# A hybrid encoder block: branch B's tiles at fixed places in the stream of projections, and four heads' meta keys as one block

## The chip, the cores and the metric

The kernel runs on one core of one Trainium2 chip. The metric is device time in microseconds (us), from the start of the program to its end. TensorE multiplies matrices, VectorE and ScalarE work on tiles in SBUF and PSUM, GpSimd on tiles in SBUF, and SyncE's queue (SP) issues all the DMAs. In the profile PE is TensorE's matmuls, PEld its weight loads, DVE VectorE, ACT ScalarE and POOL GpSimd.

## The reference

`x` has 1024 tokens of width 1024 in float32; 16 learned meta tokens are put in front, so the sequence has 1040. One layer:

```
hn     = rms_norm(h)                                   # h = [meta, x]
proj   = hn @ w_in                                     # qa ka va (512 each) qb (512) kb vb (128 each) ga gb (1024 each)
y_a    = differential attention, 4 heads, over all 1040 keys, ALiBi bias
y_b    = windowed attention, 8 query heads on 2 key/value heads of width 64 (4 heads share one):
         each query sees the 16 meta keys and the real keys within 128 positions;
         softmax with a learned sink in the denominator
merged = sigmoid(ga) * (y_a @ w_ba) + sigmoid(gb) * (y_b @ w_bb)
h      = h + merged @ w_o
h      = h + (silu(hn2 @ w_gate) * (hn2 @ w_up)) @ w_down      # hn2 = rms_norm(h), d_ff 2816
out    = rms_norm(h)[16:]
```

The change concerns `y_b` and the projections around it.

## The kernel before, in words

Float32 values are split into a high and a low part (`split`: ScalarE copies the high part, VectorE or GpSimd subtracts), and a product is three matmuls: high by high, high by low, low by high.

**The stream of projections.** `project_steps` makes 128 columns of `proj` from transposed, normed tokens (`hT_hi`, `hT_lo`), in chunks of tokens. One step is three matmuls for one of eight blocks of the contraction; after the eighth, the chunk leaves PSUM (three banks, tag `pp`). A chunk of qa has 512 tokens (16 steps for 1024). The chunks of va and ka have 384, 384 and 272 (24 steps), in ka of the last head 272 first. `prep` loads and splits a weight block; `ensure(n)` sees that n blocks are prepared ahead. The V projections pass through `vt` and are transposed later, four blocks of 128 tokens at a time (`turning_v`, one call every eight steps of the next projection). The order is kb, the first half of qb, vb; then qa, va, ka of heads 0 and 1; the second half of qb; qa, va, ka of heads 2 and 3.

**Branch B.** Group g (0 and 1) has four heads and eight tiles of 128 queries. `attend_b(g, t, qb)` does one tile:
- Scores: for each of its four heads two matmuls into PSUM (`bps`, two banks). The keys are up to three blocks of 128, each with the 16 meta keys behind it: 432 columns, at the edge tiles (0 and 7) 288. VectorE adds the bias and takes the minimum (`bmn`), ScalarE takes Exp and sums (`bdn`), VectorE adds the sink and takes the reciprocal, and GpSimd scales the four heads by it (L343).
- GpSimd copies the meta columns, twice side by side, into `md`, a zeroed tile with 128 columns for each head (`bmd`, L347).
- `finish`: for each key block four transposes, one for each head, into PSUM (`bpt`), ScalarE's high copy and VectorE's low one (`btr`), and two value matmuls of 512 columns (four heads by 128 queries) into `bpy`. Then the meta block in the same way: four transposes of `md`, a high and a low copy side by side in rows 0 to 31, and one value matmul with block 8 of `vb`, which holds V of the meta keys twice. The result is added up and stored to `yb_d`.

`units_b` writes tile t + 1's scores ahead of tile t's `finish`.

**Order.** Most of the program is ordered by a planner, which lays the instructions of each engine on a simulated timeline and takes those written first first. In `manual_schedule(engines=...)` an engine keeps the order in which the program is written. Before, GpSimd is in hand order from the second half of qb to the first gate weights, and TensorE from branch A on. Ahead of that the planner chose: it put pieces of branch B between matmuls of the projections by itself.

**Beside it on GpSimd.** `token_sums(c)` forms, for c from 0 to 3, ten sums of 128 by 512 of the tokens for the gate products (a Strassen scheme), and `keep` splits and stores four of them (`ts_d`). `weight_sums(n)` forms four sums of gate weights of 128 by 256 and stores them (`ws_d`), two calls for each tile of group 1 (`sums_of`).

After the last projection come the first gate products (L717, 72 matmuls of 512 columns), and then branch A's attention with the other gate products between its tiles (L737, L796).

Of the kernel before, what the change touches and what calls it, by code (L numbers as in the profile page):

```python
# [9 lines left out]
F32 = mybir.dt.float32  # L10
# [9 lines left out]
P = 128  # L20
# [53 lines left out]
def encoder_block(ctx: ExitStack, tc: tile.TileContext, x, meta, norm_mix, w_in, lq1, lk1, lq2, lk2,  # L74
# [7 lines left out]
    def f32(ap):  # L82
        return ap.bitcast(F32)
# [13 lines left out]
    def bank(p, tag, name, bufs):  # L97
        return p.tile([P, 512], F32, tag=tag, name=name, bufs=bufs)
# [140 lines left out]

    def project_v(col, name, evac):  # L240
        vt = vtpool.tile([P, L + NM], F32, tag="vt", name=f"vt_{name}", bufs=1)
        project(col, K_CHUNKS, name, lambda ps, at, n: nc.scalar.copy(vt[:, at:at + n], ps))
        nc.vector.tensor_copy(vt[:, L:L + NM], vt[:, S:L])

        def turn():
            for b in range(3):
                nb = 4 if b < 2 else 1
                kp = P if b < 2 else 2 * NM
                pt = pp_bank(f"pv_{name}_{b}").rearrange("p (c t) -> p c t", c=4)
                for i in range(nb):  # L250
                    k = 4 * b + i
                    nc.tensor.transpose(pt[:kp, i, :], vt[:, k * P:k * P + kp], ident)
                evac(pt[:kp, :nb, :], 4 * b, nb, kp)
                yield

        turning_v[:] = [turn()]
# [13 lines left out]
    vb = [(bpool if g else vtpool).tile([P, 9, P], F32R, tag=("q1", "vb")[g], name=f"vb{g}", bufs=1) for g in range(BG)]  # L270
    mds = [bpool.tile([P, 4, P], F32, name=f"bmd{i}") for i in range(2)]
    for i in range(2):
        nc.gpsimd.memset(f32(vb[i])[:, 8, :], 0.0)
        nc.gpsimd.memset(mds[i], 0.0)

# [32 lines left out]

    def project_qb(g, qb):
        for jj in range(2):  # L310
            ensure(1)
            for _ in qb_steps(g, qb, jj):
                pass
            ensure(W_BUFS - 1)

    def attend_b(g, t, qb):
        nm = f"{g}_{t}"
        b0, b1 = max(t - 1, 0), min(t + 2, NT)
        nb = b1 - b0
        W = nb * 144  # L320
        j0 = b0 - t + 1
        tb = tbx[:, j0:j0 + nb, :].rearrange("p j k -> p (j k)")
        st = bpool.tile([P, 4, 432], F32, tag="bs", name=f"bs_{nm}", bufs=2)
        mn = small.tile([P, 4], F32, tag="bmn", name=f"bmn_{nm}")
        dn = small.tile([P, 4], F32, tag="bdn", name=f"bdn_{nm}")
        es = small.tile([P, 4], F32, tag="bes", name=f"bes_{nm}")
        hs = slice(4 * g, 4 * g + 4)
        for r in range(4):
            ps = bank(psum1, "bs", f"bps_{nm}_{r}", 2)
            for v in range(2):  # L330
                nc.tensor.matmul(ps[:, :W], qb[:, r, t * P:(t + 1) * P],
                                 kb[g][:, v, b0:b1, :].rearrange("p b k -> p (b k)"), start=(v == 0), stop=(v == 1))
            nc.vector.tensor_tensor_reduce(st[:, r, :W], ps[:, :W], tb, 2.0 ** -(4 * g + r + 1), nsink[:, 4 * g + r:4 * g + r + 1],
                                           ALU.add, ALU.min, mn[:, r:r + 1])
        nc.vector.tensor_tensor(es, mn, sinkb[:, hs], ALU.add)
        for r in range(4):
            nc.scalar.activation(st[:, r, :W], st[:, r, :W], AF.Exp, bias=mn[:, r:r + 1], scale=-1.0,
                                 accum_out=dn[:, r:r + 1])
        nc.scalar.activation(es, es, AF.Exp)
        nc.vector.tensor_tensor(dn, dn, es, ALU.add)  # L340
        nc.vector.reciprocal(dn, dn)  # L341
        for r in range(4):
            nc.gpsimd.tensor_scalar(st[:, r, :W], st[:, r, :W], dn[:, r:r + 1], 1.0, ALU.mult, ALU.mult)  # L343

        md = mds[t % 2]
        own = (t - b0) * 144 + P
        nc.gpsimd.tensor_copy(md[:, :, 0:2 * NM].rearrange("p r (a k) -> p r a k", a=2),  # L347
                              st[:, :, own:own + NM].unsqueeze(2).broadcast_to([P, 4, 2, NM]))

        def finish():  # L350
            py = bank(psum1, "by", f"bpy_{nm}", 1)
            blocks = [(k, P, (k - b0) * 144) for k in range(b0, b1)] + [(8, P, (t - b0) * 144 + P)]
            for k, kp, o in blocks:
                pt = bank(psum1, "bt", f"bpt_{nm}_{k}", 2).rearrange("p (r t) -> p r t", r=4)
                for r in range(4):
                    nc.tensor.transpose(pt[:kp, r, :], st[:, r, o:o + P] if k < 8 else md[:, r], ident)  # L356
                tr = bpool.tile([P, 2, 4, P], F32R, tag="btr", name=f"btr_{nm}_{k}", bufs=4)
                nc.scalar.activation(tr[:kp, 0], pt[:kp], AF.Copy)
                lo = tr[:, 1] if k < 8 else tr[:NM, 0]
                nc.vector.tensor_tensor(lo, pt[:lo.shape[0]], f32(tr[:lo.shape[0], 0]), ALU.subtract)  # L360
                for hl in range(2 if k < 8 else 1):
                    nc.tensor.matmul(py, vb[g][:kp, k, :], tr[:kp, hl].rearrange("p r t -> p (r t)"),  # L362
                                     start=(k == b0 and hl == 0), stop=(k == 8))
# [5 lines left out]
        return finish  # L369

# [91 lines left out]
    early += [(p_kb, DC), (p_q0, DC), (p_q1, DC)]  # L462
    advance(100)
    dist = acon.tile([P, 1920], F32, name="dist")
    tbx = acon.tile([P, 3, 144], F32, name="tbx")
# [34 lines left out]


    first_b = [attend_b(0, t, qb) for t in range(2)]
    project_v(C_VB, "vb", vb_evac)
    flush_v()
# [5 lines left out]
    def token_sums(c):  # L510
# [16 lines left out]
        tt(t1, t1, low, ALU.add)  # L527
        keep(5, t1)
        t3, t2 = new(3), new(2)
        tt(t3, part(0, 1, 1), part(0, 0, 1), ALU.subtract)  # L530
        tt(t2, part(1, 1, 1), part(1, 0, 1), ALU.subtract)
        tt(t3, t3, t2, ALU.add)
        keep(7, t3)
        tt(t2, t3, part(0, 0, 0), ALU.add)
        tt(t2, t2, part(1, 0, 0), ALU.add)
        keep(6, t2)
        t4 = new(4)
        tt(t4, part(0, 1, 0), t2, ALU.subtract)
# [3 lines left out]
    def project_a(h):  # L542
# [16 lines left out]

        project(C_QA + h * P, Q_CHUNKS, f"qa{h}", evac_split(-(2.0 ** (2 * h - 1)), q_consume))  # L560
        project_v(C_VA + h * P, f"va{h}", va_evac)
        project(C_KA + h * P, K_CHUNKS if h < AH - 1 else K_CHUNKS[::-1], f"ka{h}", evac_split(None, k_consume))

    def units_b(g, qb, pending=(), extra=lambda t: None):
        pending = list(pending)
        for t in range(len(pending), NT):
            if len(pending) > 1:
                pending.pop(0)()
            pending.append(attend_b(g, t, qb))
            extra(t)  # L570
            if len(pending) > 1:
                pending.pop(0)()
        for p in pending:
            p()


    def load_sums(p, kh, half):
# [99 lines left out]

    order_pool = tc.manual_schedule(engines={mybir.EngineType.Pool})
    order_pool.__enter__()
    qb = new_qb(1)  # L680
    project_qb(1, qb)
    for n in range(2):
# [9 lines left out]

    units_b(1, qb, extra=sums_of)
    close_bpool()
# [187 lines left out]

    order_pe = tc.manual_schedule(engines={mybir.EngineType.PE})
    order_pe.__enter__()
    tiles, turning, tail = [], iter(()), []
# [626 lines left out]
```

## Time and profile before

| | |
|---|---|
| runs | 1446.01, 1449.07, 1449.72 us (median 1449.07) |
| profiled execution | 1446.1 us, span 1444.3 us |
| granted TensorE clock | 0.997 |
| busy, share of the span | TensorE 99%, weight loads 85%, VectorE 62%, ScalarE 47%, GpSimd 44% |
| normed tokens, kb and the first half of qb | up to 56 us |
| vb, both groups of branch B, the projections of branch A | 56 to 305 us, the last value matmul of branch B at 309.9 us |
| first gate products | to 322.9 us |
| branch A's attention and all that follows | to 1444.3 us |

The rows of a timeline have start, length, engine, line, operation, output<-inputs, shape and count; in brackets stands the idle time of the engine just before, with what ended it. The rows of groups have count, then busy us and mean ns, then idle us before them and what ended most of it. A mean length of a matmul is longer than its pace, since matmuls overlap.

### The profile page before, as it was taken

Reading aid. Unit: us, or ns where it says so; the run is one execution under the profiler, and the core shown is the slowest. Engines: PE = TensorE matmul, PEld = TensorE weight load, DVE = VectorE, ACT = ScalarE, POOL = GpSimd, SP = SyncE. Lnnn points to the kernel's source line nnn. Section 1 sums busy time; section 2 is a strip of 40 time slices with the busy share of each in tenths; the row PEclk is TensorE's granted clock in tenths of the full one; section 3 lists DMA queues with packets and bytes.
Section 4 is the critical chain, followed back from the end, with each engine's and each line's share of the span. In section 5 each row is a group of like instructions: output and inputs, shape, how many; then the busy total and the mean of one; then the engine's idle time right before and its main releaser. Section 6 shows DMA issues by size and latency. Waiting matters only on the chain.

```text
span 1444.3 us, 21160 instructions
## 1 busy us (share of the span) xinstructions
PE 1422.8 (99%) x7279; PEld 1221.2 (85%) x7279; DVE 899.2 (62%) x1624; ACT 679.6 (47%) x1290; POOL 641.3 (44%) x605
## 2 busy tenths in 40 slices
PE   8999999999999999999999999999999999999997
PEld 6988989988898999888888878888888888888886
DVE  7478536637697989624614966554555553787567
ACT  6366535545665656544413643333333333444454
POOL 5599127743333333334522665544544452000444
PEclk9999999999999999999999999999999999999999
DMA  8467658986557473576612534333332332964443
GB/s 244 90 209 237 193 162 265 288 281 213 190 169 257 147 227 125 190 256 209 216 34 88 152 104 161 109 102 110 102 102 96 110 102 102 331 208 140 124 129 139
DMA packets 188891, 242.41 MB, mean 168 GB/s; under 512 B 18208, under 2 KB 115936, under 8 KB 188784
## 3 DMA queue, kind: packets, MB, share of 16 engines
q1 hardware_dynamic: 188784, 241.07, 52.6%
q8 instruction: 57, 0.93, 0.3%
q14 instruction: 50, 0.41, 0.1%
HBM read 157.45 MB, written 77.00 MB: 162 GB/s over the span
## 4 chain that ended last, share of the span: by engine, by line
PE 81%; POOL 6%; DVE 5%; issue 4%; DMA 2%; ACT 1%; POOLq 0%; SPq 0%; DVEq 0%; ACTq 0%
PE pg L1293 28%; PE pd L1387 9%; PE pg L737 7%; PE po L1070 6%; PE ppa L780 6%; PE aps L796 3%; PE pp_qb L214 3%; POOL oa L118 3%; PE apy L835 3%; PE pp_ka L214 2%; PE pp_va L214 2%; PE apt L822 2%; PE pp_qa L214 2%; PE bpt L356 1%; PE bpy L362 1%
## 5 line engine op out<-in xcount | busy, mean ns | idle before, releaser
L118 POOL TENSOR_TENSOR wop<-wf,wop 128x512 fp32r<-128x512 f32 x128 | 172.6, 1353 | 165.5 <-ACT wop L117 149.6
L1293 PE MATMUL pg<-t,wop 128*128 128x512 f32 x1056 | 242.6, 389 | 0.0
L1293 PEld LDWEIGHTS pg<-t,wop 128*128 128x128 f32 x1056 | 198.3, 188 | 41.1
L1387 PE MATMUL pd<-ob,oa 128*128 128x512 f32 x924 | 209.9, 389 | 0.4 <-POOL oa L118 0.4
L1387 PEld LDWEIGHTS pd<-ob,oa 128*128 128x128 f32 x924 | 173.4, 188 | 36.8 <-POOL oa L118 0.8
L1293 PE MATMUL pg<-b,wop 128*128 128x512 f32 x792 | 185.6, 392 | 2.3 <-DVE c L1302 2.3
L1293 PEld LDWEIGHTS pg<-b,wop 128*128 128x128 f32 x792 | 149.5, 189 | 34.1 <-issue 2.4
L737 PE MATMUL pg<-hT_hi,gop 128*128 128x512 f32 x384 | 142.7, 396 | 0.0
L118 POOL TENSOR_TENSOR oa<-ra,oa 128x512 fp32r<-128x512 f32 x33 | 44.0, 1335 | 170.1 <-ACT oa L117 168.6
L117 ACT ACTIVATE wop<-wf 128x512 fp32r<-128x512 f32 x128 | 80.2, 631 | 82.9 <-PE pg L1293 48.6
L118 POOL TENSOR_TENSOR gop<-gr,gop 128x512 fp32r<-128x512 f32 x48 | 63.3, 1319 | 116.4 <-ACT gop L117 102.6
L117 ACT ACTIVATE oa<-ra 128x512 fp32r<-128x512 f32 x77 | 48.7, 632 | 105.9 <-PE pd L1387 45.1
L804 ACT ACTIVATE as<-as,amn 128x1040 f32<-128x1040 f32 x64 | 74.5, 1164 | 46.9 <-DVE amn L799 42.8
L1128 DVE TENSOR_TENSOR s<-wf,wf 128x512 f32<-128x512 f32 x22 | 25.0, 1138 | 108.1 <-DMA wf<-in_w_ff_gate_dram 58.0
L796 PE MATMUL aps<-ak,aq 128*128 128x392 f32 (+1 forms) x384 | 90.0, 330 | 1.3 <-DVE amn L799 0.6
L1070 PE MATMUL po<-woh,mT 128*128 128x512 f32 x384 | 88.0, 390 | 0.0
L1070 PEld LDWEIGHTS po<-woh,mT 128*128 128x128 f32 x384 | 71.9, 188 | 14.8
L796 PEld LDWEIGHTS aps<-ak,aq 128*128 128x128 f32 x384 | 69.6, 189 | 15.0 <-DVE amn L799 2.2
L737 PEld LDWEIGHTS pg<-hT_hi,gop 128*128 128x128 f32 x384 | 72.7, 189 | 11.2 <-DVE gk L742 0.2
L343 POOL TENSOR_SCALAR bs<-bs,bdn 128x432 f32<-128x432 f32 (+1 forms) x64 | 41.4, 666 | 85.5 <-DVE bdn L341 73.4
L737 PE MATMUL pg<-hT_lo,gop 128*128 128x512 f32 x192 | 76.0, 396 | 0.0
L807 POOL TENSOR_SCALAR as<-as,adn,neglam 128x1040 f32<-128x1040 f32 x32 | 38.8, 1214 | 62.5 <-DVE adn L805 43.9
(287 smaller groups left out, 3099.0 us busy)
## 6 DMA issues: line engine op xcount, KB each, us to landing
ra<-aop SPq DMA_DIRECT2D x77, 256.0 KB, 2.6
wf<-in_w_ff_gate_dram SPq DMA_DIRECT2D x24, 512.0 KB, 4.0
wf<-in_w_ff_up_dram SPq DMA_DIRECT2D x24, 512.0 KB, 3.9
aop<-as SPq DMA_DIRECT2D x44, 256.0 KB, 2.1
w_c<-in_w_in_dram SPq DMA_DIRECT2D x17, 512.0 KB, 5.7
aop<-c SPq DMA_DIRECT2D x33, 256.0 KB, 2.0
ts_d<-to SPq DMA_DIRECT2D x16, 512.0 KB, 3.7
gw<-in_w_in_dram SPq DMA_DIRECT2D x32, 256.0 KB, 3.9
```

The source lines that it names most:

```text
L117: nc.scalar.activation(hi, src, AF.Copy)
L118: lo_eng.tensor_tensor(lo, src, f32(hi), ALU.subtract)
L214: nc.tensor.matmul(ps[:, :n], a[:, c, :], b[:, c, at:at + n], start=(c == 0 and i == 0), stop=(c == DC - 1 and i == 2))
L343: nc.gpsimd.tensor_scalar(st[:, r, :W], st[:, r, :W], dn[:, r:r + 1], 1.0, ALU.mult, ALU.mult)
L737: nc.tensor.matmul(ps, op[:, a, c], quad(b, *act)[:, c], start=(p in (2, 5, 1) and c == 0 and i == 0), stop=(p in (2, 3, 4) and c == 3 and ...
L780: nc.tensor.matmul(ps, w[:, a, j, :], src(j, b, tk), start=(j == 0 and n == 0), stop=(j == 3 and n == 2))
L796: nc.tensor.matmul(ps[:, :n], qs[m][:, t * P:(t + 1) * P], ks[m][:, vv, k0:k0 + n], start=(vv == 0), stop=(vv == 1))
L804: nc.scalar.activation(s[m][:, 0:L], s[m][:, 0:L], AF.Exp, bias=low, scale=-1.0, accum_out=dn[:, m:m + 1])
L835: nc.tensor.matmul(py[:, cols], v[:kp, a, k, :], at_[:kp, k, b, :], start=(k == 0 and j == 0), stop=(k == 8))
L1070: nc.tensor.matmul(ps, mT[:, c, a, t * P:(t + 1) * P], wos[q, c][:, b], start=(c == 0 and n == 0), stop=(c == DC - 1 and n == 2))
L1293: nc.tensor.matmul(ps, op[:, x, c, :], b[:, y, c, :], start=(p in (1, 2, 5) and c == 0 and n == 0), stop=(p in (4, 2, 3) and c == 3 and n ...
L1387: nc.tensor.matmul(ps[u], oa[:, a, u * P:(u + 1) * P], ob[:, b, :], start=(p in (1, 2, 5) and j == 0 and k == 0), stop=(p in (2, 3, 4) and ...
```

## The change

1. TensorE keeps the written order from the vb projection on, and so does GpSimd. The planner still orders VectorE, ScalarE and SP.
2. `project`, `project_v`, `project_qb` become `stream`, `stream_v`, `stream_qb`, which yield after each step. `ensure` for the next weights comes in the fourth step rather than at the end.
3. `attend_b` returns two generators. `scores` yields after each head (and takes Exp of a head right behind its minimum); `turns` yields after each piece: first the transpose of the meta block and of the first key block; then for each further block its four transposes and the values of the block before; last the values of the last block and of the meta block, and the store.
4. `plan(g, t, base)` lays a tile's scores at steps base - 14, -12, -10, -8 of the stream and its pieces at base, + 4, + 8 and (inner tiles) + 12. Group 0 has base 16t + 4 from the first step of qa of head 0 on, its first tile's scores lying in steps 12 to 18 of vb; group 1 has base 182 + 13t. `along` walks the streams, 288 steps in all, and calls what is due.
5. `token_sums` yields after each kept sum, and its 16 pieces lie at steps 5, 13, 21 and so on. The weight sums of tile t lie at step 182 + 13t - 7.
6. Group 1's tiles are written among the projections of heads 2 and 3, no longer ahead of them. The vb transposes are called at once behind vb, as before.
7. `md` holds, for the four heads, 32 columns each (the 16 meta columns twice), 128 in all: one transpose for the tile. The result is copied to SBUF, and for head r the rows 32r to 32r + 31 go into columns of head r of `diag`, an otherwise zeroed tile: a high copy by ScalarE, and a low one by VectorE over the first 16 of these rows. Block 8 of `vb` holds V of the meta keys eight times (`vb_meta`), and one matmul over 128 rows gives all four heads.

```diff
-    def project(col, chunks, name, evac):
+    def stream(col, chunks, name, evac):
         ensure(1)
         for i, _ in enumerate(project_steps(col, chunks, name, evac)):
             if i % DC == V_AT and turning_v:
                 next(turning_v[0], None)
-        ensure(W_BUFS - 1)
+            if i == 3:
+                ensure(W_BUFS - 1)
+            yield
...
+        if name == "vb":
+            meta = bpool.tile([P, P], F32, tag="by1", name="vb_meta", bufs=2)
+            nc.vector.tensor_copy(meta.rearrange("p (a k) -> p a k", a=8), vt[:, S:L].unsqueeze(1).broadcast_to([P, 8, NM]))
...
     def attend_b(g, t, qb):
...
+        def scores():
...
+            for r in range(4):
+                nc.gpsimd.tensor_scalar(st[:, r, :W], st[:, r, :W], dn[:, r:r + 1], 1.0, ALU.mult, ALU.mult)
+            md = held["md"] = bpool.tile([P, 4, 2, NM], F32, tag="bmd", name=f"bmd_{nm}", bufs=2)
+            nc.gpsimd.tensor_copy(md, st[:, :, own:own + NM].unsqueeze(2).broadcast_to([P, 4, 2, NM]))
+            yield
+
+        def turns():
+            st, md, dg, trs = held["st"], held["md"], diag[:, t % 2], {}
...
+            pt = bank(psum1, "bt", f"bpt_{nm}_8", 2)[:, 0:P]
+            nc.tensor.transpose(pt, md.rearrange("p r a k -> p (r a k)"), ident)
+            sc = bpool.tile([P, P], F32, tag="bsc", name=f"bsc_{nm}", bufs=2)
+            nc.scalar.copy(sc, pt)
+            turn(b0)
+            for r in range(4):
+                hi, lo = slice(32 * r, 32 * r + 32), slice(32 * r, 32 * r + NM)
+                nc.scalar.activation(dg[hi, r], sc[hi], AF.Copy)
+                nc.vector.tensor_tensor(dg[lo, r], sc[lo], f32(dg[lo, r]), ALU.subtract)
+            yield
+            for k in range(b0 + 1, b1):
+                turn(k)
+                value(k - 1)
+                yield
+            value(b1 - 1)
+            nc.tensor.matmul(py, vb[g][:, 8, :], dg.rearrange("p r t -> p (r t)"), start=False, stop=True)
...
-    first_b = [attend_b(0, t, qb) for t in range(2)]
-    project_v(C_VB, "vb", vb_evac)
+    order_pe = tc.manual_schedule(engines={mybir.EngineType.PE})
+    order_pe.__enter__()
+    order_pool = tc.manual_schedule(engines={mybir.EngineType.Pool})
+    order_pool.__enter__()
+    diag = bpool.tile([P, 2, 4, P], F32R, tag="bys", name="diag", bufs=1)
+    nc.gpsimd.memset(f32(diag), 0.0)
+    tiles_b = {(0, t): attend_b(0, t, qb) for t in range(NT)}
+    for i, _ in enumerate(stream_v(C_VB, "vb", vb_evac)):
+        if i in (12, 14, 16, 18):
+            next(tiles_b[0, 0][0])
     flush_v()
...
+    def plan(g, t, base, scores=True):
+        sc, tu = tiles_b[g, t]
+        for i in range(4 if scores else 0):
+            events.setdefault(base - 14 + 2 * i, []).append(sc)
+        for i in range(4 if 0 < t < NT - 1 else 3):
+            events.setdefault(base + 4 * i, []).append(tu)
...
-    units_b(0, qb, first_b)
-    for c in range(2):
-        token_sums(c)
-    project_a(0)
-    token_sums(2)
-    project_a(1)
-    token_sums(3)
+    for t in range(NT):
+        plan(0, t, 16 * t + 4, t > 0)
+    pieces = [token_sums(c) for c in range(4)]
+    for n in range(16):
+        extras[8 * n + 5] = lambda g=pieces[n // 4]: next(g, None)
+    along(project_a(0))
+    along(project_a(1))
...
-    units_b(1, qb, extra=sums_of)
+    for t in range(NT):
+        tiles_b[1, t] = attend_b(1, t, qb)
+        plan(1, t, 182 + 13 * t)
+        extras[182 + 13 * t - 7] = lambda t=t: sums_of(t)
+    along(project_a(2))
+    along(project_a(3))
     close_bpool()
...
-    project_a(2)
-    project_a(3)
```

More of the change, by code (lines that the diff above doesn't have):

```diff
@@ L251, in turn @@
                     k = 4 * b + i
-                    nc.tensor.transpose(pt[:kp, i, :], vt[:, k * P:k * P + kp], ident)
+                    nc.tensor.transpose(pt[:kp, i, :], vt[:, k * P:k * P + kp] if b < 2 else meta, ident)
                 evac(pt[:kp, :nb, :], 4 * b, nb, kp)
@@ L318, in attend_b @@
         b0, b1 = max(t - 1, 0), min(t + 2, NT)
-        nb = b1 - b0
-        W = nb * 144
+        W = (b1 - b0) * 144
         j0 = b0 - t + 1
[L322 to L343, printed above, removed]
@@ L345, in attend_b @@
-        md = mds[t % 2]
-        own = (t - b0) * 144 + P
-        nc.gpsimd.tensor_copy(md[:, :, 0:2 * NM].rearrange("p r (a k) -> p r a k", a=2),
-                              st[:, :, own:own + NM].unsqueeze(2).broadcast_to([P, 4, 2, NM]))
-        def finish():
+        own = (t - b0) * 144 + P
+        held = {}
+        def scores():
+            tb = tbx[:, j0:j0 + b1 - b0, :].rearrange("p j k -> p (j k)")
+            st = held["st"] = bpool.tile([P, 4, 432], F32, tag="bs", name=f"bs_{nm}", bufs=2)
+            mn = small.tile([P, 4], F32, tag="bmn", name=f"bmn_{nm}")
+            dn = small.tile([P, 4], F32, tag="bdn", name=f"bdn_{nm}")
+            es = small.tile([P, 4], F32, tag="bes", name=f"bes_{nm}")
+            for r in range(4):
+                ps = bank(psum1, "bs", f"bps_{nm}_{r}", 2)
+                for v in range(2):
+                    nc.tensor.matmul(ps[:, :W], qb[:, r, t * P:(t + 1) * P],
+                                     kb[g][:, v, b0:b1, :].rearrange("p b k -> p (b k)"), start=(v == 0), stop=(v == 1))
+                nc.vector.tensor_tensor_reduce(st[:, r, :W], ps[:, :W], tb, 2.0 ** -(4 * g + r + 1), nsink[:, 4 * g + r:4 * g + r + 1],
+                                               ALU.add, ALU.min, mn[:, r:r + 1])
+                nc.scalar.activation(st[:, r, :W], st[:, r, :W], AF.Exp, bias=mn[:, r:r + 1], scale=-1.0,
+                                     accum_out=dn[:, r:r + 1])
+                if r < 3:
+                    yield
+            nc.vector.tensor_tensor(es, mn, sinkb[:, 4 * g:4 * g + 4], ALU.add)
+            nc.scalar.activation(es, es, AF.Exp)
+            nc.vector.tensor_tensor(dn, dn, es, ALU.add)
+            nc.vector.reciprocal(dn, dn)
+            for r in range(4):
[3 more added lines that the diff above has]
+            yield
@@ L351, in finish, with turn, value @@
+        def turns():
+            st, md, dg, trs = held["st"], held["md"], diag[:, t % 2], {}
             py = bank(psum1, "by", f"bpy_{nm}", 1)
-            blocks = [(k, P, (k - b0) * 144) for k in range(b0, b1)] + [(8, P, (t - b0) * 144 + P)]
-            for k, kp, o in blocks:
+            def turn(k):
+                o = (k - b0) * 144
                 pt = bank(psum1, "bt", f"bpt_{nm}_{k}", 2).rearrange("p (r t) -> p r t", r=4)
                 for r in range(4):
[L356 to L363, printed above, removed]
+                    nc.tensor.transpose(pt[:, r, :], st[:, r, o:o + P], ident)
+                tr = trs[k] = bpool.tile([P, 2, 4, P], F32R, tag="btr", name=f"btr_{nm}_{k}", bufs=4)
+                nc.scalar.activation(tr[:, 0], pt, AF.Copy)
+                nc.vector.tensor_tensor(tr[:, 1], pt, f32(tr[:, 0]), ALU.subtract)
+            def value(k):
+                for hl in range(2):
+                    nc.tensor.matmul(py, vb[g][:, k, :], trs[k][:, hl].rearrange("p r t -> p (r t)"),
+                                     start=(k == b0 and hl == 0), stop=False)
+            pt = bank(psum1, "bt", f"bpt_{nm}_8", 2)[:, 0:P]
[3 more added lines that the diff above has]
+            turn(b0)
+            for r in range(4):
+                hi, lo = slice(32 * r, 32 * r + 32), slice(32 * r, 32 * r + NM)
+                nc.scalar.activation(dg[hi, r], sc[hi], AF.Copy)
+                nc.vector.tensor_tensor(dg[lo, r], sc[lo], f32(dg[lo, r]), ALU.subtract)
+            yield
+            for k in range(b0 + 1, b1):
+                turn(k)
+                value(k - 1)
+                yield
+            value(b1 - 1)
+            nc.tensor.matmul(py, vb[g][:, 8, :], dg.rearrange("p r t -> p (r t)"), start=False, stop=True)
@@ L368, in finish @@
                               y1.rearrange("p (r s) -> p r s", r=4))
-        return finish
+            yield
+        return scores(), turns()
     qb = new_qb(0)
@@ L558, in va_evac, with along @@
             nc.sync.dma_start(va_d[h][:kp, :, k0:k0 + nb, :], f32(vs)[:kp, :, :nb, :])
[L560 to L574, printed above, removed]
+        yield from stream(C_QA + h * P, Q_CHUNKS, f"qa{h}", evac_split(-(2.0 ** (2 * h - 1)), q_consume))
+        yield from stream_v(C_VA + h * P, f"va{h}", va_evac)
+        yield from stream(C_KA + h * P, K_CHUNKS if h < AH - 1 else K_CHUNKS[::-1], f"ka{h}", evac_split(None, k_consume))
+    at_step, events, extras = [0], {}, {}
+    def plan(g, t, base, scores=True):
[4 more added lines that the diff above has]
+            events.setdefault(base + 4 * i, []).append(tu)
+    def along(steps):
+        for _ in steps:
+            at_step[0] += 1
+            for what in events.pop(at_step[0], ()):
+                next(what, None)
+            if at_step[0] in extras:
+                extras.pop(at_step[0])()
     def load_sums(p, kh, half):
```

30 lines of the change are left out of this document (14 added, 16 removed).

## The prediction, made before the change was run

> **What bounds the kernel now.** I read the page first, then busy time by stretches of 36 us, then the groups between 60 and 360 us, then the timeline there.
>
> ```profile
> span 1444.3 us, 21160 instructions
> PE 1422.8 (99%) x7279; PEld 1221.2 (85%) x7279; DVE 899.2 (62%) x1624; ACT 679.6 (47%) x1290; POOL 641.3 (44%) x605
> ...
> 108.00:144.00 36.00, 35.81 (x206) 32.01 (x205) 29.11 (x55) 22.37 (x52) 35.18 (x31) 1.00 0.79 233
> 252.00:288.00 36.00, 36.00 (x210) 32.51 (x209) 21.65 (x49) 20.54 (x48) 28.57 (x41) 1.00 0.94 288
> ```
>
> The columns of the stretches are length, then busy us of PE, PEld, DVE, ACT and POOL, then clock. Where the change works (some 56 to 310 us) TensorE is never idle for long, although GpSimd is almost full from 108 to 144. So the planner already mixes branch B into the projections, and there is little left to fill. What can be won is TensorE work that goes away; what can be lost is any new wait of TensorE. Busy is no measure of pace, so I take costs from start to start:
>
> ```profile
> L356 PE MATMUL bpt<-ident,bmd 128*128 128x128 f32 x64 | 10.4, 272 | 0.0
> 60.27 0.34 PE L214 MATMUL pp_vb<-hT_lo,wh_c 128*128 128x384 f32 x1
> 62.90 0.33 PE L214 MATMUL pp_vb<-hT_hi,wh_c 128*128 128x384 f32 x1
> 65.11 0.29 PE L214 MATMUL pp_vb<-hT_lo,wh_c 128*128 128x272 f32 x1
> 67.89 0.29 PE L214 MATMUL pp_vb<-hT_hi,wl_c 128*128 128x272 f32 x1
> 73.28 0.40 PE L214 MATMUL pp_qa<-hT_hi,wh_c 128*128 128x512 f32 x1
> 78.17 0.82 PE L356 MATMUL bpt<-ident,bs 128*128 128x128 f32 x6
> 85.14 0.55 PE L331 MATMUL bps<-kb,qb 128*128 128x432 f32 x2
> 85.53 0.63 PE L362 MATMUL bpy<-btr,vb 128*128 128x512 f32 x2
> 92.42 1.04 PE L356 MATMUL bpt<-ident,bs 128*128 128x128 f32 x8
> 93.21 0.42 PE L214 MATMUL pp_va<-hT_hi,wh_c 128*128 128x384 f32 x1
> 93.47 0.34 PE L214 MATMUL pp_va<-hT_lo,wh_c 128*128 128x384 f32 x1
> ```
>
> A step of the stream is three matmuls. At 512 columns 21 of them take 4.89 us (73.28 to 78.17): 0.233 each, 0.70 a step. At 384 columns 15 take 2.63 (60.27 to 62.90): 0.53 a step. At 272, 22 take 2.78 (65.11 to 67.89): 0.38. A head's scores, two matmuls, take 0.39 (85.14 to 85.53). Eight transposes take 0.79 (from 92.42), and the matmul behind them 0.26 in place of 0.175: 0.88 for eight, 0.11 each. A matmul of values has 512 columns: 0.233. So a piece with four transposes and two value matmuls is 0.90, and a tile's last piece, three value matmuls, 0.70.
>
> **Part 1: meta keys as one block (gain).** The 64 transposes of bmd in the first row become 16. 48 x 0.11 = 5.3 us of TensorE, on the path all through. The value matmul of block 8 stays one of 512 columns.
>
> ```profile
> L358 ACT ACTIVATE btr<-bpt 128x512 fp32r<-128x512 f32 x60 | 33.7, 590 | 13.5 <-PE bpt L356 13.0 <-ACT bs L337 0.2
> L293 ACT ACTIVATE vb<-pv_vb 128x256 fp32r<-128x256 f32 x4 | 1.4, 360 | 0.0
> ```
>
> ScalarE gets five small copies a tile, each under the 0.36 of a copy of 256 columns, in place of one of 0.59: at most +1.2 a tile. VectorE gets four small subtractions for one of 512 columns, about even. I put both at nothing: ScalarE is busy 20 to 22 of 36 us, and the diagonal is used two or three pieces later, over 3 us. If that cover went, the last piece of a tile would wait up to 1 us.
>
> **Part 2: what the planner lost (gain, given back at the same place).**
>
> ```profile
> 69.84 0.63 PE L331 MATMUL bps<-kb,qb 128*128 128x432 f32 x2
> 72.78 0.67 PE L331 MATMUL bps<-kb,qb 128*128 128x432 f32 x2 [0.46 <-DVE bmn L333]
> ```
>
> From the first of these pairs of scores to qa0 (73.28) there are 3.44 us. Five pairs lie there, the last of them at 72.78, less a vb transpose: 5 x 0.39 = 1.95 would do, so 1.5 are lost, because nothing stands between the pairs. By hand the second tile's scores lie inside qa0 and this goes. But the vb transposes now come at once behind the vb stream, with nothing between. They wait for the last copy of vt and for the eightfold copy of the meta rows, and qa0 needs the first of three banks back: two copies of 0.36 and two subtractions like them after the first four transposes, some 1.4 with the hand-overs, of which 0.6 lie beside the other five transposes. I take 1.5 (bounds 0.5 to 2.5), which cancels the gain. Elsewhere gaps like 36 - 35.81 give some 0.5 more. Parts 1 and 2 together: 5.3 + 0.5 = 5.8.
>
> **Part 3: fixed places (loss).** In the stream a tile's fourth scores come 8 steps before its first turning piece, and that opens with the transpose of md. Md needs everything of the tile: fourth scores, VectorE's reduce, ScalarE's Exp, the sum and the reciprocal, four scalings and the md copy on GpSimd. TensorE is in hand order, so if md is late the whole stream behind it is late, and all that the stream feeds. The quickest such chain of 432 columns, and a loaded one:
>
> ```profile
> 274.37 0.56 PE L331 MATMUL bps<-kb,qb 128*128 128x432 f32 x2
> 277.12 2.43 POOL L343 TENSOR_SCALAR bs<-bs,bdn 128x432 f32<-128x432 f32 x4 [2.33 <-PE bpy L362]
> 279.62 0.29 POOL L347 COPY bmd<-bs 128x128 f32<-128x128 f32 x1
> ...
> 248.46 0.55 PE L331 MATMUL bps<-kb,qb 128*128 128x432 f32 x2
> 253.52 3.40 POOL L343 TENSOR_SCALAR bs<-bs,bdn 128x432 f32<-128x432 f32 x4
> 256.98 0.29 POOL L347 COPY bmd<-bs 128x128 f32<-128x128 f32 x1
> L343 POOL TENSOR_SCALAR bs<-bs,bdn 128x432 f32<-128x432 f32 x48 | 33.6, 720 | 9.5 <-DVE bdn L341 3.2 <-PE pp_va L214 2.9 <-PE bpy L362 2.3
> L343 POOL TENSOR_SCALAR bs<-bs,bdn 128x288 f32<-128x288 f32 x16 | 7.8, 506 | 76.0 <-DVE bdn L341 70.2 <-ACT btr L358 5.9
> ```
>
> From the issue of the fourth scores to the end of md: 5.54 (274.37 to 279.91) and 8.81 (248.46 to 257.27). In the kernel before nothing hurries after md, so the loaded one cost nothing there. I take 6.6, nearer the quick end: the first three heads are now done well before, but VectorE and ScalarE are 57 to 81% full in the stretches above, so over five hand-overs about 1 us of queueing is to be expected. An edge tile (288 columns) has scalings of 0.51 instead of 0.72, four of them 0.9 less: 5.7.
>
> What the places leave is the pair itself (0.39), eight steps, the pieces of the tile before that fall between (0.70 in group 0; 0.70 and 0.90 in group 1 where both do), and 0.44 where four blocks of V are turned. Counted through the streams (qa 16 steps of 0.70; va and ka 16 of 0.53 and 8 of 0.38):
> Group 0, tiles 1 to 7: 5.3, 4.7, 5.7, 5.4, 6.0, 4.7, 5.7. Short of the need by 1.3, 1.9, 0.9, 1.2, 0.6, 1.9, 0: 7.8 us.
> Group 1, tiles 0 to 7: 4.9, 4.9, 6.7, 5.6, 7.5, 6.4, 5.6, 5.6. Short by 0.8, 1.7, 0, 1.0, 0, 0.2, 1.0, 0.1: 4.8 us.
> For example group 0, tile 2: scores at step 28, turned at 36, 4 x 0.53 + 4 x 0.38 = 3.6, + 0.39 + 0.70 = 4.7. Together 12.6 us of TensorE waits, with bounds of 2.7 (need 5.54, edges 4.64) and 21 (need 7.2, edges 6.3).
>
> ```profile
> L118 POOL TENSOR_TENSOR wl_c<-w_c,wh_c 128x1024 fp32r<-128x1024 f32 x6 | 14.4, 2407 | 0.8 <-ACT wh_c L117 0.8
> L530 POOL TENSOR_TENSOR ta<-hT_hi 128x512 f32<-128x512 f32 x3 | 3.9, 1288 | 0.0
> L610 POOL TENSOR_TENSOR gs<-gw 128x256 f32<-128x256 f32 x16 | 11.8, 738 | 12.4 <-DMA ws_d<-gs 12.3
> ```
>
> Hidden, at nothing: the token sums move to behind one tile's scalings and before the next one's. Two pieces, five sums of 1.29, are 6.5, scalings and md 3.2, a weight split in most gaps 2.4: 12.1 of GpSimd for some 13 us of stream with a tile in it, so it just fits. In group 1 eight weight sums of 0.74 (5.9), the 12.3 us of waits for ws_d's stores over eight tiles (1.5) and 3.2 make 10.6 for some 11.5. If either doesn't fit, the excess goes into md's lateness one to one, which is rival B. The weight loads and splits start in the fourth step of a stream and have the rest of it. Values come four steps after their turn. The last tile of group 1 ends 7 steps and the 72 first gate matmuls (72 x 0.233 = 16.8 us) ahead of branch A, so A's loads on SP's queue do not come late.
>
> **Sum**, against the profiled execution's own 1446.1 us (span 1444.3): -5.8 + 12.6 = +6.8, so 1452.9. The three runs lie between 1446.0 and 1449.7 with a median of 1449.07; the profiled one is at their low end, and the range takes that in.
>
> **The clock, a rule weighed.**
>
> ```profile
> 24.15 0.50 PE L214 MATMUL pp_qb<-hT_hi,wb_qbx 128*128 128x256 f32 x2 [1.53 <-DVE wb_qbx L118]
> 24.00:26.00 2.00, 1.85 (x15) 1.85 (x16) 2.00 (x5) 0.85 (x3) 0.74 (x2) 1.00 0.64 152
> 338.03 1.64 PE L822 MATMUL apt<-ident,as 128*128 128x128 f32 x9 [1.94 <-DVE as L810]
> 338.00:340.00 2.00, 1.97 (x11) 1.88 (x12) 1.85 (x9) 1.68 (x5) 1.29 (x2) 0.66 1.05 407
> 340.00:342.00 2.00, 2.00 (x7) 1.71 (x6) 1.94 (x6) 1.40 (x4) 1.17 (x1) 0.50 1.07 408
> ```
>
> After an idle stretch of 1.94 us the granted clock was 0.66 and 0.50 for two stretches of 2 us: 0.68 + 1.00 = 1.7 us lost. After one of 1.53 it stayed at 1.00. My waits of 1.9 lie at that edge, so the forecast adds nothing and a rival does.
> The Trainium skill (TensorE: Matmul & The Clock Gate, "Why this matters for your kernels") allows idle gaps up to about 3 us before the clock is halved. By that rule no wait here costs clock and the sum stays at 1452.9; the gap of 1.94 us above speaks against it.
>
> **Rivals.** "No change" means within 0.3%, 4.3 us, about what a measurement of this kernel can tell.
> A, faster: the chain runs at its quickest on every tile, since a waiting TensorE feeds ScalarE and VectorE less. Waits of 2.7: -5.8 + 2.7 = -3.1, 1443.0. With no wait of a tile and none at the vb turn either it is -7.3, 1438.8. It turns from loss to gain where the waits are under 5.8. For it: 5.54 was reached. Against: by one chain, others took up to 8.8. 0.30.
> B, GpSimd becomes the bound: 35.18 of 36 us in one stretch before, and scalings at 3.40 in place of 2.43 on a loaded tile. Need 7.2: 21 - 5.8 = +15.2, 1461.3. 0.13.
> C, three or four waits pass the edge and halve the clock, 1.7 each: 1452.9 + 6 = 1458.9. 0.12.
> That hand order changes nothing, because TensorE is full anyway and the waits eat just what the transposes save, is 1446; I count it under A.
>
> **Numbers.** Forecast 0.45: 1452.9, its own range 1449 to 1458. Of A 0.18 lies under 1441.8 and 0.12 above; of the forecast 0.08 lies under 1450.4. So faster 0.18, same 0.20, slower 0.62. The range 1440 to 1462 leaves out about 0.1 on either side.
>
> **What would show it.** Right: 16 md transposes; TensorE waits in front of them for GpSimd's md copy, 0.5 to 2 us on nine or more tiles; from fourth scores to md about 6.6; nothing new after 345 us. Wrong: waits before md under 6 us in sum (A), GpSimd busy without a break up to md (B), clock below 1 between 70 and 310 us (C), or a difference that arises after branch A begins.

## The result, and the profile after

The changed kernel takes 1485.06 us (median of four runs, 1483.80 to 1485.48); the kernel before, 1449.39 beside it. The ratio is 1.0249, 95% interval 1.0231 to 1.0267: 36 us slower, where 1452.9 was forecast and 1462 was the upper end. The direction was right, the size was not.

The head of the page of the changed kernel, then busy time of its PE, PEld, DVE, ACT and POOL in the first two of the stretches of 36 us:

```profile
span 1483.5 us, 21108 instructions
PE 1428.8 (96%) x7231; PEld 1216.9 (82%) x7231; DVE 935.5 (63%) x1673; ACT 697.2 (47%) x1354; POOL 631.1 (43%) x602
```

```profile
72.00:108.00 36.00, 28.65 (x137) 24.42 (x138) 21.62 (x39) 15.83 (x40) 17.98 (x16) 0.95 0.41 114
108.00:144.00 36.00, 29.52 (x180) 26.65 (x179) 27.17 (x54) 22.80 (x57) 21.12 (x21) 1.00 0.48 161
```

In the second stretch TensorE was busy for 35.81 of 36 us before, and is for 29.52 now. No engine is full: GpSimd, 35.18 before, has fallen to 21.12. TensorE waits, and so does what feeds it. By the first instruction of each stage, qa of head 0 starts 1 us earlier than before (72.3 against 73.3), the second half of qb 33 us later (208.8 against 176.1), the first gate products 40 us later (345.4 against 305.0), and the end is 39.1 us later. So all of it arises in branch B, and most in group 0.

TensorE's waits there (from 56 to 346 us; us in total, times, longest):

```profile
PE bpt L374 <- POOL bmd L352: 12.5, 10, 2.4
PE bpy L370 <- DVE btr L366: 11.1, 9, 3.5
PE bps L337 <- DVE bmn L339: 6.8, 5, 2.1
PE bpy L370 <- ACT btr L365: 1.5, 2, 1.3
PE pp_qa L214 <- DVE vb L297: 1.2, 1, 1.2
PE bps L337 <- issue: 0.9, 1, 0.9
```

The first row is the forecast wait before md, at the forecast size. The second and third, 18 us behind VectorE, were not forecast at all. What VectorE does there stands at the head of its groups, and in its timeline beside GpSimd's:

```profile
L381 DVE TENSOR_TENSOR diag<-bsc,diag 16x128 fp32r<-16x128 f32 x64 | 54.3, 848 | 27.4 <-ACT diag L380 25.9
```

```profile
79.67 2.35 POOL L118 TENSOR_TENSOR wl_c<-w_c,wh_c 128x1024 fp32r<-128x1024 f32 x1 [7.37 <-ACT wh_c L117]
79.89 3.54 DVE L381 TENSOR_TENSOR diag<-bsc,diag 16x128 fp32r<-16x128 f32 x2 [7.17 <-ACT diag L380]
...
81.98 1.31 POOL L561 TENSOR_TENSOR ta<-hT_hi 128x512 f32<-128x512 f32 x1
...
83.25 1.31 POOL L562 TENSOR_TENSOR tal<-hT_lo 128x512 f32<-128x512 f32 x1
...
83.46 0.67 DVE L339 CUSTOM_DVE_ANT_0 bs<-bps,tbx,nsink 128x432 f32<-128x432 f32 x1
84.06 0.08 DVE L339 DVE_READ_ACCUMULATOR2_ANT bmn<- 128x1 f32 x1
84.06 0.69 DVE L366 TENSOR_TENSOR btr<-bpt,btr 128x512 fp32r<-128x512 f32 x1
```

The small subtractions into the diagonal, 16 rows of 128, take 848 ns each in the mean. Two of them take 3.54 us together: the second ends at 83.43, 0.14 us after GpSimd's sum that began at 81.98, and the first, by its own record, at 82.17, 0.15 us after the weight split. Behind them stand the next head's minimum and the subtraction of a tile of probabilities (L366), which TensorE's value matmul needs; that matmul stood still for 3.51 us, the longest in the row above.

### The profile page after: what moved, and what is told of

It reads as the page before. It is cut to its first block, busy times and chain, and to the rows that moved or that the text cites. A ratio compares the mean times of both kernels' runs of the same rounds, so it can differ in the third digit from the quotient of the medians.

```text
span 1483.5 us, 21108 instructions
## 1 busy us (share of the span) xinstructions
PE 1428.8 (96%) x7231; PEld 1216.9 (82%) x7231; DVE 935.5 (63%) x1673; ACT 697.2 (47%) x1354; POOL 631.1 (43%) x602
## 4 chain that ended last, share of the span: by engine, by line
PE 67%; DVE 9%; POOL 8%; issue 6%; DMA 5%; ACT 4%; SPq 0%; POOLq 0%; DVEq 0%; ACTq 0%
PE pg L1336 26%; PE pd L1430 8%; PE pg L782 7%; PE ppa L825 6%; PE po L1113 6%; PE aps L841 3%; PE pp_qb L214 3%; POOL oa L118 3%; DVE diag L381 3%; PE apy L880 3%; POOL bs L350 2%; PE apt L867 2%; DVE bs L339 1%; POOL wop L118 1%; DMA g_d<-gk 1%
## 5 line engine op out<-in xcount | busy, mean ns | idle before, releaser
L350 POOL TENSOR_SCALAR bs<-bs,bdn 128x432 f32<-128x432 f32 (+1 forms) x64 | 38.1, 615 | 116.7 <-DVE bdn L348 91.8
L1113 PEld LDWEIGHTS po<-woh,mT 128*128 128x128 f32 x384 | 71.9, 188 | 14.8
L381 DVE TENSOR_TENSOR diag<-bsc,diag 16x128 fp32r<-16x128 f32 x64 | 54.3, 848 | 27.4 <-ACT diag L380 25.9
```

The costliest lines, as they stand in the source:

```text
L381: nc.vector.tensor_tensor(dg[lo, r], sc[lo], f32(dg[lo, r]), ALU.subtract)
L1113: nc.tensor.matmul(ps, mT[:, c, a, t * P:(t + 1) * P], wos[q, c][:, b], start=(c == 0 and n == 0), stop=(c == DC - 1 and n == 2))
```

## The experiments

Two theories stood at first. P (port): the subtraction reads two tiles in SBUF (`sc`, `dg`) and waits out whatever GpSimd is running; VectorE's queue, and TensorE behind it, wait along. F (fixed places): the hand order leaves a tile too little time, and VectorE's long instructions only fill the waiting. Ratios are to the kernel before, run beside each.

**e1, the subtraction out of PSUM.** ScalarE and VectorE read the transpose's bank, with no copy between.

```diff
-            sc = bpool.tile([P, P], F32, tag="bsc", name=f"bsc_{nm}", bufs=2)
-            nc.scalar.copy(sc, pt)
...
-                nc.vector.tensor_tensor(dg[lo, r], sc[lo], f32(dg[lo, r]), ALU.subtract)
+                nc.vector.tensor_tensor(dg[lo, r], pt[lo], f32(dg[lo, r]), ALU.subtract)
```

> The changed kernel, but the meta block's small copies and subtractions read PSUM instead of the SBUF copy, so each subtraction has one SBUF input in place of two. Theory P (the subtractions with two SBUF inputs wait out GpSimd's running instruction, and VectorE's queue behind them makes TensorE wait): they fall from 0.85 to about 0.28 us each, TensorE's 18 us of waits for VectorE (btr, bmn) mostly go, md's 12.7 us stay: 1455 to 1462 us. Theory F (the fixed places are too close, the subtractions only look long because VectorE has time): within 5 us of 1485.

1465.48 us, 1.0118 (1.0103 to 1.0133): 20 us less than the changed kernel. The 64 subtractions take 287 ns each, and the waits for the minima and most of those before the values are gone; those before md stay (13.8 us). The low parts behave as P says; the time lies a little above its range.

**e2, scores four places earlier**, with the subtraction from SBUF as in the change:

```diff
-            events.setdefault(base - 14 + 2 * i, []).append(sc)
+            events.setdefault(base - 18 + 2 * i, []).append(sc)
```

> The changed kernel with every tile's scores four steps earlier, so 12 steps from the fourth scores to the first piece instead of 8. Theory P: the 12.7 us of waits for md go and the 18 us for VectorE stay, 1470 to 1475. Theory F: nearly all of the loss goes, under 1455.

1465.34, 1.0115 (1.0100 to 1.0130). The waits before md are gone, and TensorE now waits 10.4 us for VectorE's L366 and 4.7 us for ScalarE's copies of the same blocks. The time lies between the two theories: both costs are real, and each is some 20 us while the other is there.

**e3, both edits.**

> Both edits of the two runs before: low parts from PSUM, scores four steps earlier. Theory P with the waits for md as a second, separate loss: 1440 to 1447, at or a little under the kernel before, since the 48 transposes (5.3 us) stay saved. Theory F alone: no better than the earlier scores by themselves.

1454.08, 1.0043 (1.0030 to 1.0056). Missed by 7 us. Its subtractions are fast, and still TensorE waits for a bank of PSUM (groups of VectorE; waits of TensorE from 56 to 312 us):

```profile
L379 DVE TENSOR_TENSOR diag<-bpt,diag 16x128 fp32r<-16x128 f32 x64 | 18.3, 286 | 9.3 <-ACT diag L378 7.8
```

```profile
PE bpt L363 <- DVE btr L366: 6.1, 7, 2.8
```

Its timeline shows the heads of one tile's diagonal spread out, here the first three: ScalarE's copies start at 77.54, 78.93 and 80.38, and VectorE's subtractions at 77.89, 79.61 and 80.68, each engine with other work between. The bank stays taken meanwhile.

**e4, the order by hand alone**, with the meta keys as before (a transposed block for each head; here at the head of a tile's pieces, and with one buffer of `md` in place of two):

```diff
-            pt = bank(psum1, "bt", f"bpt_{nm}_8", 2)[:, 0:P]
-            nc.tensor.transpose(pt, md.rearrange("p r a k -> p (r a k)"), ident)
...
+                nc.tensor.transpose(pt[:, r, :], md[:, r], ident)
+            tm = bpool.tile([P, 4, P], F32R, tag="btm", name=f"btm_{nm}", bufs=1)
+            nc.scalar.activation(tm, pt, AF.Copy)
+            nc.vector.tensor_tensor(tm[:NM], pt[:NM], f32(tm[:NM]), ALU.subtract)
```

> The changed kernel's fixed places and hand order, but the meta keys as before: four transposes of md, one high copy and one low subtraction of 16 x 512 out of PSUM. Theory P: no small subtractions with two SBUF inputs, so like the run with low parts from PSUM plus the 5.3 us of transposes, 1460 to 1468. Theory F: the waits stay, 1485 to 1492.

1463.59, 1.0110 (1.0093 to 1.0126), waits before md 10.2 us, the time within P's range. The fixed places without the meta block cost about 16 us; the other 20 of the change come with its meta block.

**e5 and e6, the md transpose one piece later** on top of e3, and in e6 GpSimd left to the planner in group 0 as well (the last two lines):

```diff
+                if k == b0 + 1:
+                    pt = bank(psum1, "bt", f"bpt_{nm}_8", 2)[:, 0:P]
+                    nc.tensor.transpose(pt, md.rearrange("p r a k -> p (r a k)"), ident)
...
-    order_pool = tc.manual_schedule(engines={mybir.EngineType.Pool})
-    order_pool.__enter__()
```

> Low parts from PSUM and scores four steps earlier, and also the meta block's transpose moved from the first to the second turning piece. The run with both edits still waited 6.2 us before the second block's transposes, for the PSUM bank that the meta block's eight small instructions held. If that bank is what is left, these waits go and the time is 1445 to 1449, at the kernel before; if something else of group 0 is left (hand order as such), it stays within 2 us of 1454.

> The run with the meta block in the second piece, but in group 0 the planner orders GpSimd as before (hand order from the second half of qb on). If hand order on GpSimd costs because token sums no longer fill its idle time before 72 us, this is 2 to 5 us faster than the run with it; if it is needed to bring the scalings in time, it is 3 us or more slower.

1461.14, 1.0085 (1.0070 to 1.0100), and 1459.11, 1.0070 (1.0058 to 1.0082). e5 missed: it is slower than e3. e6 is 2 us under e5, at the edge of its first alternative, but the intervals overlap, so this decides nothing. The diagonal is then what comes last:

```profile
PE bpy L387 <- DVE diag L384: 9.3, 7, 3.3
```

This is e5's row; e6 has 7.9 us there. So the eight alternating instructions of a tile often end too late for its last piece. The profiled execution of e5, at 1466.05 the slowest of its six, also had a granted clock of 0.97 from 56 to 320 us, where e3's had 1.00.

**e7 and e8, the meta block alone in the planner's order**, the subtraction out of PSUM and out of SBUF:

```diff
-                    nc.tensor.transpose(pt[:kp, r, :], st[:, r, o:o + P] if k < 8 else md[:, r], ident)
+                    nc.tensor.transpose(pt[:kp, r, :], st[:, r, o:o + P], ident)
...
+            nc.tensor.transpose(pt, md.rearrange("p r a k -> p (r a k)"), ident)
```

> The kernel before, planner's order throughout, with the one-block meta keys alone and the subtractions reading PSUM. Theory P: 48 transposes of 0.11 us go and nothing new waits, 1442 to 1446, a ratio of about 0.997. Theory F says the same here.

> The same as the run before it, but with the copy to SBUF of the changed kernel, so that the 64 subtractions have two SBUF inputs. Theory P: they take about 0.85 us and VectorE's queue is late behind them, so it is slower than with PSUM by 5 us or more even in the planner's order, 1447 to 1465, unless the slack that the planner leaves behind md hides it. Theory F: no difference between the two.

1455.19, 1.0041 (1.0029 to 1.0053), and 1451.63, 1.0019 (1.0011 to 1.0028). e7 missed by 9 us. e8 lies within its range, but in the wrong order: it is 3.6 us under e7, where P had it 5 us or more over. Its subtractions are slow all the same:

```profile
L371 DVE TENSOR_TENSOR diag<-bsc,diag 16x128 fp32r<-16x128 f32 x64 | 41.0, 640 | 4.0 <-ACT diag L370 2.2
```

In the planner's order that costs less: e8 is 7 us over e11 below, which has one fast subtraction a tile, where the changed kernel is 25 us over its like in the hand order, e12. In e7 the first gate products start 7.6 us earlier than before, but then TensorE waits for the split of a weight and for a projection's result to be stored:

```profile
PE pg L727 <- POOL wl_c L118: 5.6, 1, 5.6
PE pg L727 <- DVE qk_stage L233: 3.3, 1, 3.3
```

After each of these two waits the granted clock fell to 0.50; from 296 to 360 us it was 0.87 in the mean, some 8 us lost. The waits and the clock are more than e7's whole loss. Why the split comes so late in this order was not settled.

**e10, the changed kernel without the 40 token sums** (raw parts of the tokens are split and stored in place of the sums, so the gate products are not the layer's):

```diff
-        t1, low = new(1), new("l1")
-        tt(t1, part(0, 0, 1), part(0, 0, 0), ALU.subtract)
...
-        keep(5, t1)
+        keep(5, part(0, 0, 1))
```

> The changed kernel with the 40 token sums left out: GpSimd does not run them, and raw token parts are split and stored in their place (so the gate products differ). The subtractions still read two SBUF tiles. If a subtraction waits out the GpSimd instruction that is running, the 40 in group 0, where the token sums of 1.3 us stood, fall from about 1.2 us to between 0.3 and 0.7 us each and the time comes down by 20 us or more, to 1455 to 1465; those that stand beside splits and weight sums stay slow. If the subtraction from SBUF, or its 16 rows, is slow by itself, it stays at 0.8 to 1.2 us and the time within 6 us of 1485.

1470.03, 1.0141 (1.0127 to 1.0154). The 32 subtractions between 60 and 210 us, first in the changed kernel, then in e10:

```profile
L381 DVE TENSOR_TENSOR diag<-bsc,diag 16x128 fp32r<-16x128 f32 x32 | 33.7, 1053 | 22.0 <-ACT diag L380 21.2
```

```profile
L381 DVE TENSOR_TENSOR diag<-bsc,diag 16x128 fp32r<-16x128 f32 x32 | 11.2, 349 | 12.5 <-ACT diag L380 11.5
```

The same instruction on the same tiles takes a third once GpSimd is idle beside it. In e10, 30 of these 32 meet no GpSimd instruction and take 273 to 289 ns; the two beside a weight split take 1268 and 1434. The 32 from 210 us on, beside the weight sums of about 0.75, stay at 598 (643 in the changed kernel). The ends fit too: in the changed kernel 51 of the 64 take over 0.4 us, and each of the 51 ends 0.14 to 0.15 us after a GpSimd instruction has ended. That settles P's first half, that a subtraction waits out GpSimd's instruction: neither the SBUF source nor the 16 rows are slow by themselves. The time came down by 15 us and not by the 20 expected.

**e9, e11 and e12, one subtraction a tile.** ScalarE copies the whole transposed block, VectorE forms high or low for all 128 rows in one instruction (`lowrow` is -1 in rows that hold a low part, 0 in the others), with one operand in PSUM; the bank is then free, and four ScalarE copies place the result.

```diff
+            mh = bpool.tile([P, 2, P], F32R, tag="bsc", name=f"bmh_{nm}", bufs=2)
+            nc.scalar.activation(mh[:, 0], pt, AF.Copy)
+            nc.vector.scalar_tensor_tensor(mh[:, 1], f32(mh[:, 0]), lowrow, pt, ALU.mult, ALU.add)
...
+                nc.scalar.activation(dg[rows, r], f32(mh[rows, 1]), AF.Copy)
```

e9 has this and the scores four places earlier; e12 has this alone in the changed kernel; e11 has it in the planner's order of the kernel before.

> Scores four places earlier and the meta block out of PSUM as in e3, but the four subtractions of a tile become one VectorE instruction over all 128 rows with one PSUM operand, after which four ScalarE copies place the result. The alternation of ScalarE and VectorE within a tile is gone, and the PSUM bank is free after two instructions. If e3's remaining loss sits in that alternation (its waits of 6.24 us for a bank that VectorE held), the waits of TensorE in branch B fall below 4 us and the time comes to 1446 to 1451. If it sits in VectorE's other two-operand instructions and in the fixed order itself, the time stays at e3's 1452 to 1456.

> The kernel before, in the planner's order, with the meta block alone and one subtraction a tile out of PSUM as in e9. If the 48 transposes less are worth what they take on TensorE (5.3 us) once the small instructions cost nothing, 1444 to 1447. If the end of branch B is set by the weights' sums on GpSimd and the planner's order, as e7 and e8 suggest, 1449 to 1454 whatever the block saves.

> The changed kernel with its scores where the change put them, and only the meta block's small instructions replaced by the one VectorE subtraction of e9. This is the change as the prediction priced it, with the small instructions at about nothing. If the rest of the prediction's sum is right (transposes -5.3, waits before md +12.6), the waits before md stay at 10 to 14 us and the time is 1452 to 1460, some 25 to 33 us under the changed kernel and 8 to 15 over e9. If the late scores cost more than their visible waits, as e2 against the changed kernel suggests (12.7 us of waits removed, 19.7 us saved), it is 1461 to 1466.

e9: 1444.80, ratio 0.9971 (0.9961 to 0.9982). e11: 1444.22, 0.9966 (0.9954 to 0.9979). e12: 1459.55, 1.0075 (1.0062 to 1.0089). Of e9 the head of the page, the one subtraction, and the waits; of e12 its waits:

```profile
span 1442.8 us, 21084 instructions
PE 1418.0 (98%) x7231; PEld 1216.6 (84%) x7231; DVE 896.5 (62%) x1628; ACT 693.5 (48%) x1354; POOL 636.0 (44%) x603
```

```profile
L377 DVE SCALAR_TENSOR_TENSOR bmh<-bmh,lowrow,bpt 128x128 fp32r<-128x128 f32 x16 | 5.4, 340 | 5.4 <-ACT bmh L376 5.3
```

```profile
PE pg L768 <- DVE qk_stage L235: 2.0, 1, 2.0
PE bpy L370 <- DVE btr L366: 1.5, 4, 0.5
PE pp_qa L214 <- DVE vb L297: 1.2, 1, 1.2
PE apt L873 <- DVE as L861: 0.9, 1, 0.9
PE bpy L370 <- ACT btr L365: 0.7, 1, 0.7
```

```profile
PE bpt L374 <- POOL bmd L352: 11.7, 10, 2.3
PE bpy L370 <- DVE btr L366: 4.4, 5, 1.7
PE pp_qa L214 <- DVE vb L297: 1.2, 1, 1.2
PE bpy L370 <- ACT btr L365: 1.0, 1, 1.0
```

VectorE's 54.3 us have become 5.4, TensorE's busy time is down by 4.8 us against the kernel before (1422.8 to 1418.0), and e9 and e11 beat both kernels, by 0.29% and 0.34% against before, about the 0.3% that a measurement can tell. Their intervals overlap: once the meta block is cheap, the order by hand with earlier scores and the planner's order come out alike. The first alternatives expected for e9 and e11 held (e9 ends 1 us under its range), so the meta block is worth about what its transposes take, and e7 and e8 had not measured that. e12 lies within its first range, at the upper end.

## Why the prediction was wrong

**The step that failed is "I put both at nothing" in Part 1.** It priced the four small subtractions of a tile against one of 512 columns as "about even", taking for granted that a small instruction is a short one. Even short they are not even: out of PSUM they took 0.286 us each (e3), 18 us for 64, and the 16 subtractions of before that they replace took 10.8 in all:

```profile
L360 DVE TENSOR_TENSOR btr<-bpt,btr 16x512 fp32r<-16x512 f32 x16 | 10.8, 672 | 8.2 <-ACT btr L358 8.1
```

In the changed kernel, beside a busy GpSimd, the 64 took 54.3. "The diagonal is used two or three pieces later" was true and beside the point: not the diagonal's user waited, but what was queued behind on VectorE, the next minima and the subtractions of the probabilities. From the changed kernel to e12, which differs in these small instructions alone, the ratio falls from 1.0249 to 1.0075: about 25 us. Some 19 of them come already with e1, which only reads the operands out of PSUM and drops the copy; one instruction in place of four brings the rest. The forecast was 6.8 over before and the measurement 35.7: 25 of the 29 us missed.

The trace of before had shown it (the instructions that write `bdn`: min, median and max in ns):

```profile
L340 DVE TENSOR_TENSOR bdn<-bdn,bes x16: 140/164/2342, 71.9 to 292.6; 128x4 f32<-128x4 f32 x16
L341 DVE RECIPROCAL bdn<-bdn x16: 154/178/179, 73.0 to 292.8; 128x4 f32<-128x4 f32 x16
```

The sum of two 128x4 tiles in SBUF took up to 2342 ns; the reciprocal of one never over 179. The chain of Part 3 leads through both rows, and the prediction took up neither length. The Trainium skill (SBUF — State Buffer, "Who interferes with whom") says it outright: a VectorE instruction with two SBUF inputs contends with a GpSimd instruction that reads SBUF; with one SBUF input, outside the modes that use both ports, it does not. By the same page of the Trainium skill ("SBUF: two separate sides") the one that starts first has the shared ports for its whole length, and the other is blocked. The rows agree on all counts: 1053 ns against 349 in e10, 286 out of PSUM in e3, and the ends just behind GpSimd's. The prediction weighed another rule and not this one.

**Part 1, the gain: right.** 48 transposes less were put at 5.3 us; e9 and e11 are 3.9 and 4.5 us under the runs of before beside them, with everything else about even.

**Part 2: within its bounds.** The vb turn was to take back what the planner had lost: qa of head 0 starts 1 us earlier than before, after a wait of 1.2 us for VectorE's `vb`, within the bounds of 0.5 to 2.5 given for the turn.

**Part 3: right in its row, low in its effect.** Waits before md were put at 12.6, and the chain to md at 6.6 (edge tiles 5.7). In e12 the chain, from the fourth scores' issue to the end of md, is 6.7 in the mean (edge tiles 6.0), and the waits are 11.7: so far right. The changed kernel's 12.5 is partly luck: its chain is 7.2 (edge tiles 6.0), and the prediction's own bound for a need of 7.2 (6.3) was 21 us, but TensorE's other waits lengthened what the places leave. Both kernels have ten such waits, of 0.3 to 2.4 us. And a tile that starts late seems to turn late too: e12 waits another 5.4 us before its values (4.4 and 1.0), of which e9 keeps 2.2, and the sum had nothing for them. From e12 to e9, by nothing but earlier scores, it is 14.8 us. So without the failed step the prediction's sum of +6.8 us would have met +11.6 (e12 against before, 1459.55 against 1447.97).

**Rivals.** B fell: GpSimd was less busy than before, and stood idle for 91.8 us before its scalings until VectorE's reciprocals came. C did not happen as told: there were two spells of halved clock, 1.7 us lost in each, but at a wait for values (3.51 us) and one for a minimum (2.14), and none of the waits before md, up to 2.37, brought one. A is what e9 reaches, by moving the scores, which the change did not do. "Nothing new after 345 us" held: 40.4 us are lost when the first gate products begin, 39.1 at the end.

**What stays open.** The first gate products begin 40 us late. The waits (34 us, 1 before) less the 5.3 of the transposes, with the 3.4 of the clock, make 31 of them. The rest lies in no row of waits; TensorE's busy time is 11 us more than in e9 for as many instructions, of which the clock explains 3.4.

## What to carry to other kernels

Before a VectorE instruction is called free for its size, count its operands in SBUF and look at what GpSimd runs beside it: with two, it took here what GpSimd had still to finish. In the hand order everything queued behind it paid; in the planner's order (e8) less of it showed. Read the largest duration of a short instruction, not its median; the 2342 ns in a row of 164 ended 0.02 us after a GpSimd instruction. Where a tile needs a small split, let one operand come from PSUM and make one instruction of it for all rows.

## What the runs showed of the hardware

Whether a gap of TensorE halves the clock was not decided by its length alone. At the same md transpose, e1 stood still for 2.39 us and e12 for 2.34, and only e1's clock fell. Stretches of 2 us, the granted clock being the third number from the end, of e1 and then of e12:

```profile
136.00:138.00 2.00, 0.50 (x3) 0.50 (x4) 0.00 (x0) 0.00 (x0) 1.94 (x4) 0.80 0.73 159
138.00:140.00 2.00, 2.00 (x8) 1.71 (x7) 1.01 (x3) 1.40 (x4) 1.92 (x2) 0.50 1.05 329
```

```profile
136.00:138.00 2.00, 0.97 (x7) 0.93 (x8) 0.30 (x1) 0.45 (x2) 1.94 (x4) 1.00 0.75 147
138.00:140.00 2.00, 2.00 (x11) 1.68 (x10) 0.74 (x2) 1.89 (x6) 1.92 (x3) 1.00 1.08 310
```

In e12 none of five gaps from 1.67 to 2.34 us lowered it; in the changed kernel gaps of 3.51 and 2.14 did and one of 2.75 did not. The halved spells there were some 3.4 us long each; in e7 two were twice as long. The limit of about 3 us that the prediction weighed (the Trainium skill, TensorE: Matmul & The Clock Gate, "Why this matters for your kernels") is no safe one here: the clock halved after a wait of 2.14 us as well.
